# Turning the second 256 tokens of three feature blocks by transposing transfers in place of TensorE transposes

## The chip, the cores and the metric

The kernel runs on one core of a Trainium2 chip. The time is the device time of one execution in microseconds (us), the median of three runs of the kernel before: 1074.78 us (1074.22 to 1075.33).

## The reference

One layer of a residual block for 512 frames of width 1024, all in float32:

```python
for l in range(DEPTH):                                    # DEPTH = 1
    x = x + 0.5 * swiglu(rms_norm(x, ffn1_norm[l]), ffn1_w1[l], ffn1_w3[l], ffn1_w2[l])
    ...                                                   # two token mixers, gates, w_out
    x = x + 0.5 * swiglu(rms_norm(x, ffn2_norm[l]), ffn2_w1[l], ffn2_w3[l], ffn2_w2[l])
return rms_norm(x, final_norm)

def swiglu(h, w1, w3, w2):
    return (jax.nn.silu(h @ w1) * (h @ w3)) @ w2          # 1024 -> 2816 -> 1024
```

The change touches the two SwiGLU stages only: the part that makes `silu(h @ w1) * (h @ w3)`, 2816 features for 512 tokens, and hands it to the product with `w2`.

## The kernel before, in words

**Order of the program.** The first SwiGLU stage fills the first quarter of the execution, the mixers the middle, and the second SwiGLU stage the last quarter. Both stages are one class, `Wide`, so what the change does happens once near 110 to 235 us and once more near 843 to 968 us. Within the stage each engine's instructions run in the order in which the code issues them.

**The wide product.** Of the 2816 features, the first 256 are made apart and the other 2560 in five blocks `b` = 0 to 4 of 512 features. A block is made of seven products `n` = 0 to 6 (a scheme of seven products for a 2 by 2 split of tokens and input rows, with sums of weights taken on the way). A product (b, n) has 24 matrix products of 128 by 512: two halves `h` of the weights, two groups `i` of 128 tokens, two slices `k` of 128 input rows, and three products each, since every float32 operand is split into a rounded part and a rest (`hi` and `lo`). From the third block on the order is (b,0), (b-1,4), (b-1,3), (b,1), (b,2), (b,6), (b,5), and the stage ends with (4,4), (4,3). `m` counts the products in this order.

**Weights.** After half `h` of product `m`, `weight(m + 2, h)` splits the weights of two products later: a cast on ScalarE (ACT) into a ring of four places (`sraw`, `swhi`) and a subtraction on VectorE (DVE) for the rest (`sraw`, `extra`, `swlo`). Then it starts the next transfer into the buffer that was just read: a plain load on SyncE's queue (`cc`, and others), or a load that adds to what is there on GpSimd's queue (POOL).

**Gating and turning.** `finish` combines the products in PSUM into two tiles, `u[0]` for the first 256 tokens and `u[1]` for the second 256, gates them, and leaves 128 tokens on the partitions by 512 features. The product with `w2` (class `Seven`) wants features on the partitions: `hidden(j)`, tiles named `rl` and `rh`. There are two ways to turn:

- *By transfers*: `apart` splits each float32 into its two 16-bit words with two ACT copies (128 by 1024 words) into a scratch tile (`p`, or the silu tile `sa` for the second half), and two transposing DMAs on SyncE's queue write them back, turned, into `u`. `joined` puts the words together with four ACT copies of 128 by 512 words, at the place in the order that `joins` names.
- *By TensorE (PE)*: `turn_half` turns `u[1]` with eight transposes of 128 by 128 into two PSUM banks, and four ACT copies of 128 by 256 take them out.

Before the change the first 256 tokens of blocks 0 to 3 and the second 256 of block 0 go by transfers; the second 256 of blocks 1, 2 and 3 go by `turn_half`, after the first half of (b,2) of the block that follows; block 4 goes by TensorE (`turn`) at the stage's end.

**The stage's end.** During (4,6) and (4,5) ACT and DVE also prepare the first operands of `Seven` from the turned features: `one` casts them, and `second(1)` subtracts `rh` from `rl` for feature tiles 8 to 15, whose second 256 tokens come from blocks 1, 2 and 3. After (4,3), PE turns block 4's `u[0]` and `u[1]` between the first products with `w2`.

In the rows below all of these run through one helper at line 103; tiles tell them apart. In the trace "P" is a PSUM bank.

Of the kernel before, what the change touches and what calls it, by code (L numbers as in the profile page):

```python
# [19 lines left out]
P = 128  # L20
T = 512
# [61 lines left out]
def kernel(  # L83
# [24 lines left out]
    dve, act, pe = [Queued(e, False) for e in (nc.vector, nc.scalar, nc.tensor)]  # L108
# [18 lines left out]
    def tmp(name, shape=(P, T), dt=F32, tag="t", **kw):  # L127
        return tp.tile(list(shape), dt, tag=tag, name=name, **kw)


    ident = cp.tile([P, P], F32, name="ident")
# [42 lines left out]
    def mm3(ps, whi, wlo, xhi, xlo, first, last, onto=False):  # L174
        pe.matmul(ps, whi, xhi, start=first, stop=False, skip_group_check=onto)  # L175
        pe.matmul(ps, whi, xlo, start=False, stop=False, skip_group_check=onto)  # L176
        return pe.matmul(ps, wlo, xhi, start=False, stop=last, skip_group_check=onto)  # L177
# [322 lines left out]
    KH, TH, LO, HI = KF // 2, T // 2, slice(0, D // 2), slice(D // 2, D)  # L500
# [149 lines left out]
    class Wide:  # L650
# [139 lines left out]
                cols = slice(half * TH, (half + 1) * TH)  # L790
                act.copy(s.seven.hidden(2 + 4 * s.end + f)[:, cols], s.turns[f][:, cols])

        def turn_half(s, b):
            for f in range(4):
                for i in range(2):
                    pe.transpose(s.Y[b % 2][f // 2][:, (2 * (f % 2) + i) * P:][:, :P], s.u[1][:, i, f * P:(f + 1) * P], ident[:])
            for f in range(4):
                act.copy(s.seven.hidden(2 + 4 * b + f)[:, TH:T], s.Y[b % 2][f // 2][:, f % 2 * TH:][:, :TH])

        def apart(s, b, half):  # L800
            for i in range(2):
                parts, words = (s.sa if half else s.p[b])[i].bitcast(U16), s.u[half][:, i].bitcast(U16)
                act.copy(parts.rearrange("p (s c) -> p s c", s=2), words.rearrange("p (c s) -> p s c", s=2))
                nc.sync.dma_start(words.rearrange("p (a t) -> p a t", t=P), parts, transpose=True)
# [104 lines left out]
        def blocks(s, pa, pb, more):  # L909
            sv, end, nrm = s.seven, s.end, s.nrm  # L910
            raw = [[t[k][:, 0:TH] for k in range(KD)] for t in (nrm.hi, nrm.lo)]
            soon = {(0, 0): ((s.sums, 1),), (0, 6): ((s.low, 1),), (1, 6): ((s.low, 2),), (0, 1): ((s.low, 4),),
                    (0, 2): ((s.low, 5),), (0, 5): ((s.low, 3),)}
            todo = {(0, 0): ((s.gated, 0),),
                    (1, 0): ((s.cast, 1), (s.sums, 2)),
                    (0, 6): ((s.cast, 2), (s.sums, 4), (s.back, 0)),
                    (1, 6): ((s.cast, 4), (s.sums, 5), (s.hidden, 1, pa[:], pb[:])),
                    (0, 1): ((s.cast, 5), (s.gated, 1)),
                    (0, 2): ((s.cast, 3),),
                    (0, 5): ((s.cast, 0),),  # L920
                    (0, 3): ((s.low, 0), (s.cast, 6)),
                    (1, 2): ((s.low, 6),),
                    (2, 5): ((sv.second, 0),), (3, 2): ((sv.two, 0),),
                    (end, 0): ((sv.operand, 0, 0),), (end, 2): ((sv.operand, 0, 1),), (end, 6): ((sv.one, 0),),
                    (end, 5): ((sv.second, 1), (sv.one, 1)), (end, 4): ((sv.two, 1), *[(s.plain, sv.O[i], s.residual[i]) for i in range(2)])}
            for at, steps in more.items():
                todo[at] = tuple(todo.get(at, ())) + steps
            joins = {}
            for m, (b, n) in enumerate(s.order):
                apart = n == 4 and (b < EARLY or b == end)  # L930
                early = m < 2 * EARLY
                ps = s.X[b % 2] if n in (0, 2, 3, 5) or early else s.X[(b + 1) % 2] if n == 6 or apart else s.Y[b % 2]
                onto = n in (2, 3, 5) or (n == 6 and early) or (n == 4 and not apart)
                last = m + 2 >= len(s.order)
                if last:
                    sv.slots += s.ring[2 * m % 4:2 * m % 4 + 2]
                for h in range(2):
                    wh, wl = s.ring[(2 * m + h) % 4]
                    for i in range(2):
                        for k in range(2):  # L940
                            c = slice(i * P, (i + 1) * P)
                            if early:
                                qh, ql = [t[4 * (n > 0) + 2 * h + k][:, c] for t in raw]
                            else:
                                qh, ql = [t[:, 2 * h + k, c] for t in s.q[n]]
                            mm3(ps[i][:], qh, ql, wh[:, k], wl[:, k], not onto and h + k == 0, h + k == 2, onto)
                    if b > 1 and (n, h) == (2, 0):
                        s.turn_half(b - 1)
                    if h == 1:
                        if m == len(s.order) - 1:  # L950
                            s.turns = dict(zip((0, 2, 1, 3), s.Y[end % 2] + s.X[1 - end % 2]))
                            act.activation(s.sa[0], ps[0][:], AF.Silu)
                            act.activation(s.sa[1], ps[1][:], AF.Silu)
                            s.turn((0, 2), 0)
                            for i in range(2):
                                dve.tensor_tensor(s.u[1][:, i], s.u[1][:, i], s.sa[i], op=ALU.mult)
                            sv.operand(0, 2)
                        else:
                            s.finish(m)
                    if h == 1:  # L960
                        for f, *a in soon.get((b, n), ()):
                            f(*a)
                    if not last:
                        s.weight(m + 2, h)
                    elif len(sv.slots) == 2:
                        sv.weight(0, h)
                    elif h == 0:
                        sv.slots.insert(2, s.last)
                        sv.weight(0, 2)
                        sv.weight(0, 3)  # L970
                    else:
                        sv.weight(0, 4)
                    if (m, h) in joins:
                        s.joined(*joins[m, h])
                if n == 4 and b < end or (b, n) == (0, 3):
                    s.apart(b, int(n == 3))
                    joins[m + 3, 0] = b, int(n == 3)
                s.gate(m)
                for f, *a in todo.get((b, n), ()):
                    f(*a)  # L980
            sv.slots.append(tuple(tmp("g5", (P, 1, T), F32R)[:] for _ in range(2)))
            sv.junk = [tmp(f"osq{i}")[:] for i in range(2)]
            sv.weight(0, 5)
            sv.run()
# [121 lines left out]
    with ExitStack() as mx:  # L1106
# [292 lines left out]
        for t in range(C - 1):  # L1399
            n, m = t + 1, C - 1 - t  # L1400
# [820 lines left out]
```

## Time and profile before

| | before |
|---|---|
| median of three runs | 1074.78 us |
| the profiled execution | 1075.51 us |
| its span, first to last instruction | 1073.8 us |
| PE busy | 1064.3 us (99%) |
| DVE busy | 829.5 us (77%) |
| ACT busy | 706.7 us (66%) |
| POOL busy | 224.5 us (21%) |
| granted TensorE clock | 1.000 |
| DMA traffic | 184.48 MB, mean 172 GB/s |

Stretches of 38 us of the two stages (times from the span's start): from 110 to 148 us PE is busy 38.00 us, DVE 25.75, ACT 24.58, and the DMA engines have a share of 0.93; from 186 to 224 us 38.00, 29.92, 26.04 and 0.84; from 224 to 262 us 37.79, 35.77, 26.34 and 0.97. A share of DMA near or above 1 means that all 16 engines had packets all the time.

How to read the rows: a row of the timeline gives the start, the duration, the engine, the line, the operation, what is written and read, the shape, and in brackets how long the engine stood idle before it and what ended that. SPq is SyncE's queue, and its row is the issue of a transfer. In the view of the DMA engines the window is cut into 40 equal slices, with a digit (tenths busy) and GB/s for each.

### The profile page before, as it was taken

What the parts mean: (1) busy time and instruction counts of PE and PEld (TensorE: products, weight loads), DVE (VectorE), ACT (ScalarE), POOL (GpSimd) and SP (SyncE); (2) the same over time, 40 slices, a digit from 0 to 9 for tenths busy, and PEclk for the clock granted to TensorE, in tenths of its full rate; (3) what the DMA queues carried; (4) which work ended last, traced back from release to release, by engine and by line L of the source; (5) the groups of instructions that cost most, each with busy time, mean ns of one, the idle gap of its engine ahead of it and who ended that gap; (6) DMA issues with size and microseconds to landing.
All of it is one profiled execution on the core that took longest, in us unless ns stands there. A gap on an engine that the chain in (4) does not pass through costs nothing.

```text
span 1073.8 us, 16805 instructions
## 1 busy us (share of the span) xinstructions
PE 1064.3 (99%) x6266; PEld 872.7 (81%) x6266; DVE 829.5 (77%) x1155; ACT 706.7 (66%) x1115; POOL 224.5 (21%) x275
## 2 busy tenths in 40 slices
PE   9999999999999999999999999999999999999997
PEld 7888888888887887888788787888888888888886
DVE  7997676789865698888777777876798766689874
ACT  6768756776555666545888876554578757676654
POOL 1221220134203201412000121135311212114210
PEclk9999999999999999999999999999999999999999
DMA  7989988889945443444312344667979979879972
GB/s 209 264 188 232 226 178 227 196 194 187 233 129 168 116 111 98 129 136 118 89 46 73 100 129 153 188 168 181 290 168 226 196 205 200 201 216 202 233 191 79
DMA packets 171664, 184.48 MB, mean 172 GB/s; under 512 B 41662, under 2 KB 107774, under 8 KB 171582
## 3 DMA queue, kind: packets, MB, share of 16 engines
q1 hardware_dynamic: 137454, 111.82, 35.3%
q0 software_dynamic: 33392, 70.14, 34.1%
q10 hardware_dynamic: 736, 1.45, 0.4%
q8 instruction: 49, 0.80, 0.3%
q14 instruction: 33, 0.27, 0.1%
HBM read 163.51 MB, written 12.52 MB: 164 GB/s over the span
## 4 chain that ended last, share of the span: by engine, by line
PE 78%; issue 12%; DVE 4%; DMA 2%; POOL 2%; ACT 2%; POOLq 0%; DVEq 0%; ACTq 0%; SPq 0%
PE P L103 21%; PE P L175 6%; PE P L176 6%; PE P L177 6%; PE pgt L103 5%; PE l L103 3%; PE spot L103 3%; PE pq L103 3%; PE ppj L103 2%; PE pk L175 2%; PE pk L177 2%; PE pk L176 2%; PE pw L176 1%; PE pw L177 1%; PE pw L175 1%
## 5 line engine op out<-in xcount | busy, mean ns | idle before, releaser
L103 PE MATMUL P<-sraw,q 128*128 128x512 f32 x344 | 91.3, 389 | 0.0
L103 PEld LDWEIGHTS P<-sraw,q 128*128 128x128 f32 x344 | 64.6, 188 | 13.4
L103 PE MATMUL P<-swhi,q 128*128 128x512 f32 x224 | 71.3, 390 | 0.2 <-DVE q L103 0.2
L167 ACT CAST whi<-raw 128x1024 fp32r<-128x1024 f32 (+2 forms) x42 | 40.4, 961 | 43.7 <-issue 14.2
L103 PE MATMUL P<-sraw,wxh 128*128 128x512 f32 x200 | 67.9, 391 | 0.0
L103 PE MATMUL P<-swhi,wxh 128*128 128x512 f32 x144 | 56.8, 394 | 0.0
L103 PE MATMUL P<-swhi,wxl 128*128 128x512 f32 x144 | 56.1, 390 | 0.0
L103 PE MATMUL P<-swlo,wxh 128*128 128x512 f32 x144 | 56.1, 389 | 0.0
L168 DVE TENSOR_TENSOR wlo<-raw,whi 128x1024 fp32r<-128x1024 f32 (+2 forms) x43 | 48.4, 1126 | 9.5 <-ACT whi L167 8.3
L693 POOL DMA_DIRECT2D cb<-in_ffn_w_dram x20 | 24.1, 1207 | 144.8 <-DVE cd L103 77.5
L693 POOL DMA_DIRECT2D cd<-in_ffn_w_dram x24 | 29.3, 1221 | 116.7 <-DVE sraw L103 38.7
L103 PE MATMUL P<-sraw,wxl 128*128 128x512 f32 x136 | 53.0, 389 | 0.0
L103 PEld LDWEIGHTS P<-swhi,q 128*128 128x128 f32 x224 | 41.9, 188 | 9.3 <-DVE q L103 0.6
L103 PEld LDWEIGHTS P<-sraw,wxh 128*128 128x128 f32 x200 | 37.5, 188 | 7.7
L103 PE MATMUL P<-swlo,q 128*128 128x512 f32 x112 | 43.6, 389 | 0.0
L103 ACT COPY RD<-spot 32x128 f32<-32x128 f32 (+2 forms) x128 | 39.8, 311 | 5.3 <-PE spot L103 2.4
L103 DVE TENSOR_TENSOR u<-P,u 128x512 f32<-128x512 f32 x52 | 33.6, 682 | 7.6 <-ACT u L103 7.6
L552 POOL DMA_DIRECT2D ca<-in_ffn_w_dram x16 | 19.3, 1205 | 94.6 <-DVE swlo L103 65.6
L177 PE MATMUL pk<-xh,wlo 128*128 128x512 f32 x96 | 37.5, 392 | 1.0 <-DVE wlo L168 1.0
L175 PE MATMUL pk<-xh,whi 128*128 128x512 f32 x96 | 38.0, 396 | 0.4 <-DVE u L1254 0.4
L176 PE MATMUL pk<-xl,whi 128*128 128x512 f32 x96 | 37.5, 391 | 0.0
L177 PE MATMUL P<-swhi,wxl 128*128 128x512 f32 x96 | 37.3, 389 | 0.0
(630 smaller groups left out, 3432.3 us busy)
## 6 DMA issues: line engine op xcount, KB each, us to landing
raw<-in_w_in_dram SPq DMA_DIRECT2D x40, 512.0 KB
cc<-in_ffn_w_dram SPq DMA_DIRECT2D x36, 512.0 KB
cb<-in_ffn_w_dram POOLq DMA_DIRECT2D x36, 512.0 KB, 6.9
cb<-in_ffn_w_dram SPq DMA_DIRECT2D x32, 512.0 KB
cd<-in_ffn_w_dram POOLq DMA_DIRECT2D x32, 512.0 KB, 7.7
ca<-in_ffn_w_dram POOLq DMA_DIRECT2D x32, 512.0 KB, 8.0
ca<-in_ffn_w_dram SPq DMA_DIRECT2D x20, 512.0 KB
cd<-in_ffn_w_dram SPq DMA_DIRECT2D x18, 512.0 KB
```

Source lines behind the costliest of these rows:

```text
L103: q.last = do(*a, **kw)
L167: (hi_eng or act).copy(hi[:], raw[:])
L168: (eng or dve).tensor_tensor(lo[:], raw[:], hi[:].bitcast(F32), op=ALU.subtract)
L175: pe.matmul(ps, whi, xhi, start=first, stop=False, skip_group_check=onto)
L176: pe.matmul(ps, whi, xlo, start=False, stop=False, skip_group_check=onto)
L177: return pe.matmul(ps, wlo, xhi, start=False, stop=last, skip_group_check=onto)
L552: nc.gpsimd.dma_start(s.sum[g], src, accum_op=ALU.add)
L693: nc.gpsimd.dma_start(to, s.block(b, n, h), accum_op=ALU.add)
```

## The change

`turn_half` and its call go. In its place, for b = 2, 3 and 4, after the first half of (b,1), `apart(b - 1, 1)` issues two ACT copies of `u[1]` into `sa` and two transposing DMAs on SyncE's queue, and `joined(b - 1, 1)` runs three products later, after the first half of (b,5). In each stage this takes 24 transposes off PE and 12 copies of 128 by 256 off ACT, and adds 6 copies of 128 by 1024 words and 12 of 128 by 512 words to ACT and 6 transposing DMAs to SyncE's queue.

```diff
-        def turn_half(s, b):
-            for f in range(4):
-                for i in range(2):
-                    pe.transpose(s.Y[b % 2][f // 2][:, (2 * (f % 2) + i) * P:][:, :P], s.u[1][:, i, f * P:(f + 1) * P], ident[:])
-            for f in range(4):
-                act.copy(s.seven.hidden(2 + 4 * b + f)[:, TH:T], s.Y[b % 2][f // 2][:, f % 2 * TH:][:, :TH])
-
...
-                    if b > 1 and (n, h) == (2, 0):
-                        s.turn_half(b - 1)
...
                     if (m, h) in joins:
                         s.joined(*joins[m, h])
+                    if b > 1 and (n, h) == (1, 0):
+                        s.apart(b - 1, 1)
+                        joins[m + 3, 0] = b - 1, 1
                 if n == 4 and b < end or (b, n) == (0, 3):
                     s.apart(b, int(n == 3))
                     joins[m + 3, 0] = b, int(n == 3)
```

Nothing else moves: on every engine the other instructions keep their order. Three places show what does, all in the last round, b = 4, of the first stage. On ACT, around (4,1) and (4,2), where `swhi<-cc` are the casts of (4,6)'s weights and `sraw<-cb` the cast of (4,5)'s:

```order
 L103 CAST sraw<-cd_380 128x1024
 L103 CAST swhi<-cc_363 128x1024
+L103 COPY sa_455<-u_385 128x1024
+L103 COPY sa_456<-u_385 128x1024
 L103 CAST swhi<-cc_364 128x1024
-L103 COPY rl_372<-P_501 128x256
-L103 COPY rh_375<-P_501 128x256
-L103 COPY rl_373<-P_502 128x256
-L103 COPY rh_376<-P_502 128x256
 L103 CAST sraw<-cb_381 128x1024
```

The four copies out of PSUM are gone, and the two that split words stand one half product earlier, between the two casts. On ACT again, around (4,5), where `wxh<-rl` is an operand for `w2`, `sraw<-cd` the cast of (4,3)'s first half of weights, and `u<-P` takes (4,5) out of PSUM:

```order
 L103 CAST wxh_507<-rl_371 128x1024
 L103 CAST sraw<-cd_379 128x1024
+L103 COPY rl_372<-u_385 128x512
+L103 COPY rh_375<-u_385 128x512
+L103 COPY rl_373<-u_385 128x512
+L103 COPY rh_376<-u_385 128x512
 L103 COPY u_385<-P_495 128x512
 L103 COPY u_385<-P_496 128x512
```

The four copies of `joined` stand ahead of the two that free PSUM after (4,5), and so ahead of all that ACT does up to the stage's end. On SyncE's queue at the same round, the changed kernel's rows (before, the same rows without the two that read `sa`; `u_384<-p` belongs to the first 256 tokens):

```order
L797 DMA_TRANSPOSE u_384<-p_503 128x8x128
L797 DMA_TRANSPOSE u_384<-p_504 128x8x128
L797 DMA_TRANSPOSE u_385<-sa_455 128x8x128
L690 DMA cc_363<-in_ffn_w_dram 128x2x512
L797 DMA_TRANSPOSE u_385<-sa_456 128x8x128
L690 DMA cc_364<-in_ffn_w_dram 128x2x512
L555 DMA cb_381<-in_ffn_w_dram 128x2x512
```

One transposing DMA now stands ahead of each of the two `cc` loads, which bring the weights of (4,4).

## The prediction

> **What bounds the kernel now.** I read the page, then TensorE's waits, then the stretch of the last rounds of blocks, then the rows of ACT, DVE and the DMA engines there. The profiled execution took 1075.51 us, 0.7 us over the median of 1074.78; I sum against its span and put the difference on the median.
>
> ```profile
> span 1073.8 us, 16805 instructions
> PE 1064.3 (99%) x6266; PEld 872.7 (81%) x6266; DVE 829.5 (77%) x1155; ACT 706.7 (66%) x1115; POOL 224.5 (21%) x275
> PE P L103 <- DVE u L103: 0.4, 2, 0.2
> 186.00:224.00 38.00, 38.00 (x174) 31.54 (x173) 29.92 (x32) 26.04 (x36) 4.82 (x4) 1.00 0.84 215
> ```
>
> The rows are from the page, from PE's waits and from the busy times by stretch. PE sets the time: in the last round of the first stage (third number of the window row) it is busy all 38 us. Among its few waits is one by place: twice, once a stage, it waits for DVE's `u`. That is the stage's end, and PE reaches it with nothing to spare. So time taken off PE counts only as far as the stage's end gets earlier too.
>
> **What leaves PE.**
>
> ```profile
> 123.39 1.04 PE L103 MATMUL P<-ident,u 128*128 128x128 f32 x8
> 124.50 0.39 PE L103 MATMUL P<-extra,wxh 128*128 128x512 f32 x1
> 124.73 0.39 PE L103 MATMUL P<-sraw,wxl 128*128 128x512 f32 x1
> L103 PE MATMUL P<-ident,u 128*128 128x128 f32 x40 | 5.8, 274 | 0.2 <-DVE u L103 0.2
> ```
>
> The first three rows are PE's timeline in round b = 2, the last is the group of all transposes of `u` in the first stage. One `turn_half` is eight transposes. From 123.39 to 124.50 lie 1.11 us; one product of the steady pace (124.50 to 124.73, 0.23) is in it, so a call costs 0.88 us. Of the 40 transposes of a stage 24 go: 3 x 0.88 = 2.64 us, in two stages **5.3 us**. That is the gross gain, on the path.
>
> **What ACT loses and gets.**
>
> ```profile
> L103 ACT COPY rh<-P 128x256 f32<-128x256 f32 x10 | 3.7, 386 | 1.2 <-PE P L103 1.2
> L103 ACT COPY sa<-u 128x1024 uint16<-128x1024 uint16 x2 | 2.0, 1055 | 0.0
> L103 ACT COPY rl<-u 128x512 uint16<-128x512 uint16 x10 | 6.9, 692 | 0.0
> 204.14 0.71 ACT L103 COPY rl<-u 128x512 uint16<-128x512 uint16 x1
> 204.71 0.72 ACT L103 COPY rh<-u 128x512 uint16<-128x512 uint16 x1
> ```
>
> These are ACT's groups in the first stage and two rows of its timeline. A round loses four copies of 0.39 us and gets two of about 1.05 and four of 0.69 that follow each other every 0.57 (204.14 to 204.71), so 2.3 us for the four of `joined`. ACT is busy 26 of 38 us, and the weights it casts are for two products later. In the second and third round (b = 2, 3) I cost all of it at nothing: that lead covers it, and if it were gone each round would lose up to the 2.3 us. In the last round there is no such cover.
>
> **The chain at the stage's end.**
>
> ```profile
> 209.48 1.06 ACT L103 CAST swhi<-cc 128x1024 fp32r<-128x1024 f32 x1
> 210.74 1.05 ACT L103 CAST swhi<-cc 128x1024 fp32r<-128x1024 f32 x1 [0.20 <-PE P L103]
> 212.81 1.23 ACT L103 ACTIVATE p<-p 128x512 f32<-128x512 f32 x2 [1.02 <-DVE p L103]
> 214.88 1.05 ACT L103 CAST sraw<-cd 128x1024 fp32r<-128x1024 f32 x1
> 215.83 1.06 ACT L103 COPY u<-P 128x512 f32<-128x512 f32 x2
> 216.78 1.06 ACT L103 CAST sraw<-cd 128x1024 fp32r<-128x1024 f32 x1
> 220.87 1.06 ACT L103 CAST wxh<-rl 128x1024 fp32r<-128x1024 f32 x1 [3.03 <-DVE rl L103]
> 210.96 1.22 DVE L103 TENSOR_TENSOR swlo<-cc,swhi 128x1024 fp32r<-128x1024 f32 x1
> 212.09 1.28 DVE L103 TENSOR_TENSOR p<-P,p 128x512 f32<-128x512 f32 x2
> 218.49 1.21 DVE L103 TENSOR_TENSOR extra<-cd,sraw 128x1024 fp32r<-128x1024 f32 x1
> 219.62 1.22 DVE L103 TENSOR_TENSOR rl<-rl,rh 128x1024 f32<-128x1024 f32 x1
> 221.96 1.23 DVE L103 TENSOR_TENSOR wxl<-rl,wxh 128x1024 fp32r<-128x1024 f32 x1 [1.12 <-ACT wxh L103]
> 231.18 1.28 DVE L103 TENSOR_TENSOR u<-u,sa 128x512 f32<-128x512 f32 x2
> 232.52 0.55 PE L103 MATMUL P<-ident,u 128*128 128x128 f32 x3 [0.21 <-DVE u L103]
> ```
>
> These are the timelines of ACT, DVE and PE in the last round; read them backwards. PE's transposes at 232.52 wait for `u<-u,sa` (231.18 to 232.46). From 221.96 to there DVE has no idle stretch, and at 221.96 it had waited for ACT's `wxh`, which had waited 3.03 us for DVE's `rl<-rl,rh`, ended at 220.84. That follows `extra<-cd`, whose cast ACT makes at 216.78 after the two copies at 215.83. So whatever moves the end of `rl<-rl,rh` moves PE. From the silu at 212.81 to 220.84 it is 8.03 us.
>
> `joined` now stands between 214.88 and 215.83 and moves the cast at 216.78 by 2.3 us. Its end goes from 217.84 to 220.14 on this scale, while DVE was ready for it at 218.49; so 1.65 us are added, and silu to the end of `rl<-rl,rh` becomes 9.7 us.
>
> When can the silu start? By PE's lead and the four PSUM copies that ACT no longer makes (I estimate 0.6 of their 1.5 us), at best 212.81 - 2.64 - 0.6 = 209.5; then `rl<-rl,rh` ends at 219.2, 1.6 us earlier than before, in place of 2.64. ACT keeps its order, however: ahead of the silu stand both casts of `cc`, and these need the loads that now have a transposing DMA in front of each.
>
> **The DMA queue.**
>
> ```profile
> L804 SPq DMA_TRANSPOSE u<-sa x4: 1237/1310/2420, 91.8 to 827.3; - x4
> 198.63 3.09 SPq L690 DMA_DIRECT2D cc<-in_ffn_w_dram  x2
> DMA  0899999999999999999417888679779980006797
> DMA  9999999999999999999989753332122101000009
> DMA  9979997756322312111109198301888998999996
> DMA packets 1676, 0.43 MB, mean 213 GB/s; under 512 B 1673, under 2 KB 1673, under 8 KB 1676
> DMA packets 414, 0.80 MB, mean 398 GB/s; under 512 B 25, under 2 KB 25, under 8 KB 414
> q0 software_dynamic: 544, 1.05, 59.3%
> q1 hardware_dynamic: 2537, 1.36, 52.3%
> q0 software_dynamic: 372, 0.73, 107.5%
> q1 hardware_dynamic: 15, 0.00, 0.6%
> ```
>
> On SyncE's queue a transpose waits for its ACT copy, and the `cc` load, the second transpose, the second `cc` load and then `cb` stand behind it. An issue takes 1.3 us in the median (first row), so `cc` goes out that much later than at 198.63; that is hidden by the time the loads lie in a full queue.
>
> The first DMA row is 190 to 230 us in slices of 1 us: from about 191 to 209 all engines are full. The second (207 to 211, slices of 0.1) thins out from 209.3; I put the end of the second `cc` load at 209.7. The third is the same place of the second stage (942 to 946): thin from 942.8, last packets at 943.9. The `cc` loads are the last of that queue, so what is put ahead of them delays them.
>
> In the last rows q0 is POOL's queue and q1 SyncE's. A transposing DMA moves 128 x 1024 words of 2 bytes, 0.262 MB in 1024 packets of 256 B. The trace has no such transfer at this place, so I bound it. Alone on the engines (155.6 to 157.6 us, the row of 1676 packets) they pass at 213 GB/s: a pair costs 0.524 / 213 GB/s = **2.5 us**. Mixed with adding loads (836 to 848 us; q0 544 packets, q1 2537): the 1.05 MB of q0 take 5.8 us at the pace of 198 to 202 us (372 packets, 0.73 MB in 4 us), the 0.84 MB of q1 that is not turned 2.1 us at the 398 GB/s of plain loads alone (206.9 to 208.9 us), and of 12 us some 4 are left for the pair. From below, at that same 398 GB/s, 1.3 us; nothing at all only if the loads need not wait for it. I take 2.5: the new transposes alternate with plain loads of their own queue, and the adding loads were issued before them.
>
> The Trainium skill (Advanced Engine Details and Errata, X-Bar Transpose) holds that transposing DMAs are as fast as ordinary ones, 350 to 400 GB/s. This trace shows 213. By the page a pair would be an estimated 1.4 us and the sum below -0.5 us.
>
> **The sum.** At (4,1) PE leads by 2 x 0.88 = 1.76, and the queue with it.
>
> First stage: second load at 209.7 - 1.76 + 2.5 = 210.4; its cast of 1.05 ends at 211.5; silu; `rl<-rl,rh` ends 9.7 later at 221.2, against 220.84: **+0.4**.
>
> ```profile
> 943.99 1.05 ACT L103 CAST swhi<-cc 128x1024 fp32r<-128x1024 f32 x1 [0.22 <-PE P L103]
> 952.85 1.22 DVE L103 TENSOR_TENSOR rl<-rl,rh 128x1024 f32<-128x1024 f32 x1
> ```
>
> Second stage: 943.9 - 1.76 + 2.5 = 944.6, the cast ends at 945.7, `rl<-rl,rh` at 955.4, against 954.07: **+1.3**. (Here the load was in time by 0.1 us only.)
>
> So PE gains 2.64 us a stage and waits 3.0 and 3.9 us there: **+1.7 us** in all, 1073.8 to 1075.5 in the span, and **1076.5 us** on the median. With S for the pair's price, the sum is 2S - 3.3 from S of about 1.
>
> **Rivals.**
>
> *The loads are not held up.* If the transposes cost `cc` under 0.6 us, `joined` alone decides: -1.6 in the first stage; in the second 943.9 - 1.76 + 1.05 + 9.7 = 952.9 against 954.07, -1.2. Sum -2.8, **1072.0 us**. For it: with q0 and q1 served in turn, `cc` would pass adding loads. Against it: in the window 198 to 202, with `cc` issued at 198.63, q0 moved 372 packets and q1 nothing but 15 tiny ones. The Trainium skill (DMA: Bandwidth & Descriptors, Queues, rings and completion order) says each engine goes round the queues that have work; by those rows the trace does not show it. Chance 0.22.
>
> *The pair costs what it cost in the mix, 4 us (slower).* Place: (4,1), where two adding loads are in flight when the first transpose is issued, as at 836 us. Then 2 x 4 - 3.3 = +4.7, **1079.5 us**. It is beyond 0.2% from S = 2.7. The Trainium skill (VectorE: DVE Perf Modes, Rules for kernel authors) advises TensorE for turning 128 by 128 where PSUM will do; that rule speaks for this rival, and the priced rows cannot exclude it. Against it: the adding loads are issued first here. Chance 0.26.
>
> *The full gain.* The chain above has slack that I don't see, and all 5.3 us arrive: **1069.5 us**. For it: in every earlier place such transfers were hidden (PE has no gap in the window row above, with such a pair in it). Against it: PE's waits at 232.52 show the chain taut. Chance 0.10.
>
> That PE isn't relieved can be left out: its rows of transposes are gone from the order.
>
> **How the numbers follow.** The forecast, 1076.5 us, has 0.42; its own range is S from 1.3 to 2.9, -0.7 to +2.5, 1074.1 to 1077.3. The range of 8 in 10 runs from 1 us under the first rival, 1071.0, to half a us above the second, 1080.0; left out are the full gain and a price above 4.3 us. A measurement of this kernel tells 0.2%, 2.1 us, from no change. Faster: the full gain 0.10 and two thirds of the first rival, 0.15: 0.25. Slower: the second rival but a little, 0.25, and the top of the forecast's range, 0.05: 0.30. The same: 0.45.
>
> **What would show it.** In the changed profile: PE's steady pace without the eight transposes, and products 0.88, 1.76, 2.64 us earlier after each round; ACT's first cast of `cc` in (4,6) idle before it, waiting for a DMA; `rl<-rl,rh` ending near 221.2 and 955.4; PE's wait for DVE's `u` grown from 0.4 us to some 7 us. If that wait stays under 2 us, the chain or the DMA price is wrong; if PE stalls in (2,4) or (3,4) instead, the cover of the earlier rounds is.

## The result, and the profile after

The changed kernel takes **1085.55 us** (median of 11 runs, 1077.5 to 1089.27); the kernel before, on the same chips, 1074.78 (also of 11). The ratio is 1.0097, with a 95% interval of 1.0077 to 1.0117: slower by some 10.8 us, outside the predicted range of 1071.0 to 1080.0. The runs of the kernel before lie within 1.1 us of each other, those of the changed kernel within 11.8 us. In all that follows, executions more than 1.5% above the fastest of their kernel (two of ten in run 2, two of four in run 5) count as slow: the ratios leave them out, the medians and ranges do not.

The profiled execution of the changed kernel took 1089.27 us, the slowest of the 11, so the trace shows the loss at its largest (3.7 us over the median); the span grew from 1073.8 to 1087.6 us. Its page and its list of PE's waits (us in all, times, longest):

```profile
span 1087.6 us, 16757 instructions
PE 1065.9 (98%) x6218; PEld 871.7 (80%) x6218; DVE 831.6 (76%) x1155; ACT 725.0 (67%) x1127; POOL 224.6 (21%) x275
PE P L103 <- DVE u L103: 6.4, 6, 2.1
PE P L103 <- DVE p L103: 4.1, 1, 4.1
PE pv L176 <- DVE wlo L168: 1.1, 1, 1.1
```

PE executes 48 matrix instructions fewer and is still busy 1.6 us longer. Waits are not the whole story, then: some of PE's work got slower.

Where the time comes in is read from instructions that both kernels have. The next two fences show four of them on PE's timeline, first of the kernel before, then of the changed one: round b = 2 of the first stage, the first product after the first stage, the start of the second stage's rounds, the first product after the second stage.

```profile
98.91 0.39 PE L103 MATMUL P<-sraw,wxh 128*128 128x512 f32 x1
237.48 0.39 PE L103 MATMUL P<-sraw,q 128*128 128x512 f32 x1
821.38 0.39 PE L103 MATMUL P<-sraw,wxh 128*128 128x512 f32 x1
970.71 0.39 PE L103 MATMUL P<-sraw,q 128*128 128x512 f32 x1
```

```profile
98.76 0.39 PE L103 MATMUL P<-sraw,wxh 128*128 128x512 f32 x1
237.60 0.39 PE L103 MATMUL P<-sraw,q 128*128 128x512 f32 x1
823.28 0.39 PE L103 MATMUL P<-sraw,wxh 128*128 128x512 f32 x1
984.24 0.39 PE L103 MATMUL P<-sraw,q 128*128 128x512 f32 x1
```

Between the first two the changed kernel loses 138.84 - 138.57 = 0.3 us, between the second and third (the middle of the program, which the change does not touch) 1.8 us, and between the last two, the second stage, **11.6 us**. The same three differences are taken of every run below.

**The second stage.** The waits of over 1 us on PE's timeline there, and the granted clock behind them (stretch, its length, PE's busy time and instructions, granted clock, share of the DMA engines, GB/s):

```profile
918.07 0.50 PE L103 MATMUL P<-swhi,q 128*128 128x512 f32 x1 [2.14 <-DVE u L103]
956.71 0.77 PE L103 MATMUL P<-swhi,q 128*128 128x512 f32 x1 [4.09 <-DVE p L103]
972.09 0.33 PE L103 MATMUL P<-ident,u 128*128 128x128 f32 x1 [1.36 <-DVE u L103]
918.00:920.00 2.00, 1.93 (x5) 0.62 1.08 265
920.00:922.00 2.00, 2.00 (x6) 0.52 1.08 313
922.00:924.00 2.00, 2.00 (x10) 1.00 1.05 404
956.00:958.00 2.00, 1.29 (x3) 0.51 1.07 395
958.00:960.00 2.00, 2.00 (x6) 0.50 0.95 285
960.00:962.00 2.00, 2.00 (x7) 0.50 0.91 350
962.00:964.00 2.00, 2.00 (x9) 0.78 1.02 411
972.00:974.00 2.00, 1.63 (x7) 0.78 0.80 92
974.00:976.00 2.00, 2.00 (x7) 0.50 0.99 176
976.00:978.00 2.00, 2.00 (x11) 0.87 0.92 136
```

The waits are 2.14 + 4.09 + 1.36 = 7.6 us. Behind each, PE's clock is at half: 6 or 7 instructions in 2 us in place of 10 or 11. PE's busy time in these stretches times the missing share of the clock is 0.73 + 0.96 + 0.63 + 1.00 + 1.00 + 0.44 + 0.36 + 1.00 + 0.26 = 6.4 us. With the 2.6 us that PE saves, 7.6 + 6.4 - 2.6 = 11.4 of the 11.6 us.

What the two longer waits hang on is seen on ACT and DVE (timelines, stage 2), and on the queues of POOL and SyncE at the last round of both stages (issues: start, time on the queue):

```profile
914.26 0.68 ACT L103 COPY rl<-u 128x512 uint16<-128x512 uint16 x1 [2.78 <-DMA u<-sa]
953.66 1.04 ACT L103 CAST swhi<-cc 128x1024 fp32r<-128x1024 f32 x1 [8.23 <-DMA cc<-in_ffn_w_dram]
956.02 1.05 ACT L103 CAST swhi<-cc 128x1024 fp32r<-128x1024 f32 x1 [1.32 <-DVE swlo L103]
954.74 1.23 DVE L103 TENSOR_TENSOR swlo<-cc,swhi 128x1024 fp32r<-128x1024 f32 x1 [7.86 <-ACT swhi L103]
955.88 1.28 DVE L103 TENSOR_TENSOR p<-P,p 128x512 f32<-128x512 f32 x2
965.55 1.22 DVE L103 TENSOR_TENSOR rl<-rl,rh 128x1024 f32<-128x1024 f32 x1
```

```profile
196.38 2.19 SPq L797 DMA_TRANSPOSE u<-sa  x1
199.48 5.86 SPq L797 DMA_TRANSPOSE u<-sa  x1
935.58 1.20 POOL L693 DMA_DIRECT2D cd<-in_ffn_w_dram  x1 [1.13 <-DVE extra L103]
935.68 2.71 SPq L797 DMA_TRANSPOSE u<-sa  x1
938.49 2.37 SPq L690 DMA_DIRECT2D cc<-in_ffn_w_dram  x1
940.91 8.73 SPq L797 DMA_TRANSPOSE u<-sa  x1
949.74 0.56 SPq L690 DMA_DIRECT2D cc<-in_ffn_w_dram  x1
```

In the second stage ACT's first cast of `cc` in (4,6) waits 8.23 us for its load; DVE's `swlo<-cc` waits for that cast, `p<-P,p` stands behind it, and PE's 4.09 us end with the first `p`. A round earlier `joined` waits 2.78 us for its transposed words, and the copies out of PSUM stand behind it: that is the wait of 2.14 us. The first `cc` load was issued at 938.49, behind the first transpose, and landed 15.1 us later, 2.1 us after that transpose. On SyncE's queue the second transpose takes 8.73 us to issue, and the second `cc` load goes out only behind it, at 949.74: 11.3 us after the first. It landed at 955.92, and until 955.97 DVE was at work for the first load's weights, so the late landing of the first load by itself explains PE's 4.09 us. In the first stage the second transpose takes 5.86 us to issue. How fast the DMA engines moved at these two places (windows of the changed kernel; granted clock, share of the DMA engines, GB/s):

```profile
200.00:202.00 2.00, 1.00 1.12 203
204.00:206.00 2.00, 1.00 1.20 174
942.00:944.00 2.00, 1.00 1.37 89
944.00:946.00 2.00, 1.00 1.44 93
946.00:948.00 2.00, 1.00 1.47 77
948.00:950.00 2.00, 1.00 0.89 79
```

The engines are busy nearly all the time at both places (a share of 0.89 or more). In the first stage they move some 170 to 200 GB/s, in the second 77 to 93 for 8 us. In these 8 us, called the collapse below, a transposing transfer and an adding load of POOL are in flight together: the adding load that was issued at 935.58 landed 16.9 us later, the transpose of 935.68 after 15.8 us.

### The profile page after: what moved, and what is told of

Read it like the earlier page. It is cut to its first block, busy times and chain, and to the rows that moved or that the text cites. A ratio compares the mean times of both kernels' runs of the same rounds, so it can differ in the third digit from the quotient of the medians.

```text
span 1087.6 us, 16757 instructions
## 1 busy us (share of the span) xinstructions
PE 1065.9 (98%) x6218; PEld 871.7 (80%) x6218; DVE 831.6 (76%) x1155; ACT 725.0 (67%) x1127; POOL 224.6 (21%) x275
## 4 chain that ended last, share of the span: by engine, by line
PE 83%; DMA 5%; DVE 5%; ACT 4%; issue 2%; SPq 0%; POOL 0%; DVEq 0%; ACTq 0%; POOLq 0%
PE P L103 30%; PE P L176 5%; PE P L177 5%; PE P L175 5%; PE pgt L103 5%; PE l L103 3%; PE spot L103 3%; PE pq L103 3%; DMA cc<-in_ffn_w_dram 2%; PE ppj L103 2%; PE pk L175 2%; PE pk L177 2%; DMA u<-sa 2%; PE pk L176 2%; PE pw L176 1%
## 5 line engine op out<-in xcount | busy, mean ns | idle before, releaser
L103 PE MATMUL P<-swhi,q 128*128 128x512 f32 x224 | 74.8, 406 | 6.5 <-DVE p L103 4.1
L103 PEld LDWEIGHTS P<-swhi,q 128*128 128x128 f32 x224 | 44.2, 198 | 17.2 <-issue 4.5
L103 PE MATMUL P<-swhi,wxl 128*128 128x512 f32 x144 | 56.5, 393 | 0.0
L103 DVE TENSOR_TENSOR swlo<-cc,swhi 128x1024 fp32r<-128x1024 f32 x20 | 24.5, 1224 | 21.3 <-ACT swhi L103 20.8
```

The source lines that it names most:

```text
L103: q.last = do(*a, **kw)
```

## Experiments

Two theories stood against each other. A: the new transfers hold up the loads that stand behind them, and PE waits for these. B: ACT's new copies come between its casts and set the end. The differences in the table are those of the four rows above, each run's against the kernel before's, in its profiled execution; medians are of 4 to 11 runs.

| kernel | median, us (range) | ratio (95%) | stage 1 | middle | stage 2 |
|---|---|---|---|---|---|
| changed | 1085.55 (1077.5-1089.3) | 1.0097 (1.0077-1.0117) | +0.3 | +1.8 | +11.6 |
| 1 without the new transfers | 1073.7 (1072.4-1075.5) | 0.9988 (0.9978-0.9998) | -1.7 | +1.8 | -1.5 |
| 2 blocks 1, 2 by transfers, 3 on PE | 1073.18 (1071.0-1091.9) | 0.9985 (0.9973-0.9997) | -1.7 | +1.6 | -0.1 |
| 3 block 3 alone by transfers | 1082.11 (1081.4-1082.5) | 1.0067 (1.0052-1.0082) | +2.7 | +2.1 | +2.7 |
| 4 a product later | 1078.05 (1077.9-1079.8) | 1.0033 (1.0020-1.0046) | +0.3 | +1.5 | +1.2 |
| 5 in effect the change again | 1100.0 (1083.3-1110.9) | none | +1.8 | +3.3 | +12.6 |
| 6 in effect 2 again | 1073.32 (1072.2-1076.9) | 0.9993 (0.9983-1.0003) | -1.8 | +1.6 | -1.8 |
| 7 kernel before with a wait | 1086.37 (1085.2-1087.7) | 1.0109 (1.0094-1.0124) | +5.8 | +0.1 | +5.3 |
| 8 as 2, PE padded | 1074.32 (1073.9-1075.7) | 0.9999 (0.9990-1.0009) | -0.2 | 0.0 | -0.2 |
| 9 behind the loads | 1074.08 (1073.2-1077.0) | 0.9995 (0.9986-1.0004) | -1.4 | +2.0 | -1.5 |
| 10 as 9, block 3 on PE | 1072.06 (1071.0-1073.2) | 0.9975 (0.9965-0.9985) | -1.8 | +0.6 | -1.8 |
| 11 as 10, PE padded | 1073.2 (1072.4-1074.0) | 0.9985 (0.9976-0.9994) | -0.8 | +0.1 | -0.8 |
| 12 transposes later by a copy | 1080.46 (1079.6-1081.7) | 1.0054 (1.0037-1.0070) | +0.5 | +1.3 | +2.5 |

**1: without the new transfers.**

```diff
-                nc.sync.dma_start(words.rearrange("p (a t) -> p a t", t=P), parts, transpose=True)
+                if move:
+                    nc.sync.dma_start(words.rearrange("p (a t) -> p a t", t=P), parts, transpose=True)
...
-                        s.apart(b - 1, 1)
+                        s.apart(b - 1, 1, False)
```

> The changed kernel without its new transposing transfers: both ACT copies of `apart` and the four of `joined` stay, `joined` reads u[1] as it stands (so the second half of three blocks is not turned, and its values are wrong). Theory A (the new transfers hold up the loads that stand behind them, and PE waits for these): 1070 to 1073 us, near the 1072.0 of the rival 'the loads are not held up', and no PE wait over 2 us. Theory B (ACT's new copies come between the casts and set the end): the time stays near that of the change, 1080 us or more. If PE's relief were worth nothing: 1075.

1073.7 us: theory A. ACT's six copies per round are there, and still the two stages come out 1.7 and 1.5 us shorter. So the transfers cost the 11.9 us between this run and the change, and ACT's copies don't. It is a little over the range expected, 1070 to 1073, for the middle takes 1.8 us back (below).

**2 and 3: which rounds.** In the one, round b = 4 keeps `turn_half`; in the other, rounds 2 and 3 do.

```diff
+                    if b > 1 and not (b < end) and (n, h) == (2, 0):
+                        s.turn_half(b - 1)
...
-                    if b > 1 and (n, h) == (1, 0):
+                    if b > 1 and (b < end) and (n, h) == (1, 0):
```

> Blocks 1 and 2 (rounds b = 2, 3) turned by transfers as in the change, block 3 (round b = 4) on PE as before. If only the last round is without cover, as the prediction had it: 2 x 0.88 us a stage stay, 1071.3 us. If round b = 3 is hit too, as the changed kernel's trace shows with PE's wait of 2.14 us before 918.07: 1074 to 1080 us, with more spread from run to run than the kernel before.

> Only block 3 (round b = 4) by transfers, blocks 1 and 2 on PE as before. If the last round alone makes the loss: 1080 us or more, nearly all that the change loses. If the loss is shared over the rounds: 1076 to 1080.

1073.18 and 1082.11 us. The last round alone loses 7.3 us (2.7 in each stage and 2.1 in the middle), two thirds of the change's loss, steadily; rounds 2 and 3 gain on balance (eight of the ten executions from 1071.0 to 1077.2). In the profile of run 3 the transposes go out 0.66 us behind the adding load in both stages, and the engines do not fall below 100 GB/s: the first ones land in 9.9 and 10.1 us. What it loses is the stage's end, twice, with the half clock behind waits of 1.91 and 2.19 us.

**4: a product later.** `apart` after (b,2) h = 0, both `cc` loads ahead of the transposes.

```diff
-                    if b > 1 and (n, h) == (1, 0):
+                    if b > 1 and (n, h) == (2, 0):
                         s.apart(b - 1, 1)
-                        joins[m + 3, 0] = b - 1, 1
+                        joins[m + 2, 0] = b - 1, 1
```

> `apart` one product later, after (b,2) h = 0, so that on SyncE's queue both `cc` loads go out ahead of the transposes and POOL's adding loads are nearly done when these are moved; `joined` stays where it is. Theory A: the loads go out as before, 1071 to 1074 us, PE's waits at the stage's end under 2 us. Theory B (ACT's copies, which stay the same): 1080 us or more. If the transposes are too late for `joined`: ACT waits for DMA u<-sa before (b,5) and the time is over 1076.

1078.05 us: neither theory's number. The third case, transposes too late for `joined`, is not it either: ACT nowhere waits for them. The executions lie within 1.9 us, but PE waits 2.14 and 2.12 us at the stages' ends. `apart`'s two ACT copies now stand at 202.56, ahead of the copies out of PSUM and of the `cc` casts, and the silu starts at 210.63 (209.30 in run 1). Place of the transfers and place of the copies had to be told apart.

**5 and 6: an attempt that changed nothing.** The copies were to stay where the change has them, and the transfers to be issued after (b,2) h = 0.

```diff
+                    if b > 1 and (n, h) == (1, 0):
+                        s.apart(b - 1, 1, send=False)
+                    if b > 1 and (n, h) == (2, 0):
+                        s.apart(b - 1, 1, copy=False)
+                        joins[m + 2, 0] = b - 1, 1
```

> As the run with the transfers behind the loads, but only the transfers come one product later (after (b,2) h = 0, behind both `cc` loads); `apart`'s two ACT copies stay after (b,1) h = 0. There these copies stood between the casts and put the silu 1.3 us later in each stage. If that was what the later place lost: 1073 to 1075.5 us, the silu in the first stage near 209.3 (as in the run without transfers) and PE's waits at the stage's end under 1.5 us. If the transfers delay the end from any place: 1077 us or more.

> Blocks 1 and 2 by transfers behind the loads (copies after (b,1) h = 0, transfers after (b,2) h = 0), block 3 on PE. If the spread of the kernel with blocks 1 and 2 by transfers ahead of the loads (1071.0 to 1091.9) came from transposes that share the DMA engines with adding loads: 1071 to 1073 us with all runs within 3 us. If the spread stays, its cause is another.

1100.0 us (1083.3 to 1110.9) and 1073.32 (1072.2 to 1076.9). Neither tests its theory. Nothing in the code ties these transfers to the loads, and in the built program they stand where they stood; SyncE's queue in run 5:

```profile
195.79 1.96 SPq L799 DMA_TRANSPOSE u<-sa  x1
197.85 0.92 SPq L690 DMA_DIRECT2D cc<-in_ffn_w_dram  x1
```

So run 5 repeats the change and run 6 repeats run 2, in the same order of every engine. What they show is the spread of one and the same order: the change and run 5 together from 1077.5 to 1092.8 us, runs 2 and 6 from 1071.0 to 1077.2, without the four executions that the ratios leave out.

**7: a wait without a transfer.** The kernel before, with eight ACT copies ahead of the silu in (4,6):

```diff
                 for t in s.p[b]:
+                    for _ in range(4 if b == s.end else 0):
+                        act.copy(t, t)
+                for t in s.p[b]:
                     act.activation(t, t, AF.Silu)
```

> The kernel before, with eight copies of p onto itself (128x512, about 0.57 us each) put ahead of the silu in (4,6) of each stage: 4.6 us of ACT on the chain of the stage's end, and nothing on the DMA side; the result stays the same. If a wait costs its length alone: two PE waits of about 4.5 us, 1083.8 us, granted clock 1.00 throughout. If PE's clock falls to half after a wait of over 2 us, as the changed kernel's trace shows from 956.04: 1.7 to 3.4 us more in each stage, 1087 to 1091 us.

The wait came out shorter than meant. PE's timeline and a window behind it:

```profile
229.61 0.33 PE L103 MATMUL P<-ident,u 128*128 128x128 f32 x1 [3.19 <-DVE u L103]
232.00:234.00 2.00, 2.00 (x9) 0.50 0.75 133
```

Two waits of 3.19 us should make about 1081 us; it took 1086.37, and the clock is at half for 3.41 us after each. The stages lost 5.8 and 5.3 us, so a wait at this place costs its length and 2.1 to 2.6 us more, with no transfer involved.

**8: as many PE instructions as before.** As run 6 (in effect run 2), with eight dummy transposes in each of the two rounds:

```diff
                         s.apart(b - 1, 1, copy=False)
+                        for f in range(8):
+                            pe.transpose(s.Y[(b - 1) % 2][f // 4][:, 8 * (f % 4):][:, :8], ident[0:8, :], ident[0:8, 0:8])
```

> As the run with blocks 1 and 2 by transfers behind the loads and block 3 on PE, but PE does eight dummy transposes of 128x8 in the two rounds, so that it executes as many instructions as the kernel before. If the wait of 1.0 to 1.4 us at pv<-wlo (465 us), which all changed kernels have and the kernel before has not, comes from where the fetch of PE's instructions (16 KB, one packet) falls beside the load raw<-in_w_in: that wait is gone, the load lands 3.9 us after its issue and not 5.4, and the time is at or under that of the kernel without the dummies although these cost PE up to 0.5 us each round. If the wait stays, it has another cause.

The wait at `pv<-wlo` is gone and the middle's difference is 0.0. The dummies cost all that PE had saved (stage 1 -0.2 in place of -1.8), so the time is 1.0 us over that of run 6, not at or under it as expected. In the load `raw<-in_w_in` before that wait, 15 of its 16 shares land within 4.0 us of the issue in both kernels; the last took 5.34 us in the changed one and 3.95 in this one (3.88 in the kernel before).

**9: behind the loads, copies early.** The transfers are tied to the last load:

```diff
+                if send:
+                    with ExitStack() if copy else tc.issue_after(loads[-1].ins):
+                        sent = nc.sync.dma_start(words.rearrange("p (a t) -> p a t", t=P), parts, transpose=True)
+                    if not copy:
+                        loads.append(sent)
...
+                    if b > 1 and (n, h) == (1, 0):
+                        s.apart(b - 1, 1, send=False)
+                    if b > 1 and (n, h) == (1, 1):
+                        s.apart(b - 1, 1, copy=False)
+                        joins[m + 3, 0] = b - 1, 1
```

> All three blocks by transfers; `apart`'s ACT copies after (b,1) h = 0 as in the change, its two transfers tied behind both `cc` loads (after (b,1) h = 1), so that on SyncE's queue the order is cc, cc, transpose, transpose, cb, cb. The silu of the first stage comes near 209.3 as in the run without transfers, and PE's waits at the stage's end fall under 1.5 us each: 1073 to 1075.5 us with runs within 3 us of each other, if the change's loss is that the transposes meet the adding loads and hold up `cc`. If the transfers delay the end from any place: 1077 us or more, or a spread as wide as the change's.

1074.08 us: **11.5 us come from where two DMA issues of a round stand**. SyncE's queue in the last round of the second stage, two DMA windows there, ACT's silu of the first stage and PE's waits for `u`:

```profile
930.41 3.21 SPq L690 DMA_DIRECT2D cc<-in_ffn_w_dram  x2
933.67 7.08 SPq L800 DMA_TRANSPOSE u<-sa  x2
936.00:938.00 2.00, 1.00 1.08 269
940.00:942.00 2.00, 1.00 1.60 107
209.31 1.23 ACT L103 ACTIVATE p<-p 128x512 f32<-128x512 f32 x2 [0.39 <-DVE p L103]
PE P L103 <- DVE u L103: 1.8, 6, 0.4
```

Both `cc` loads go out in 3.2 us, the silu starts at 209.31 (the prediction had 209.5 as the best), and PE's longest wait for `u` is 0.4 us. The transposes still take 7.1 us to issue, but only `cb` is behind them. The engines slow down here too, to 107 GB/s at 940 to 942, but for 2 us, and when the second `cc` load lands at 940.97. The transposes now go out 3.9 to 4.3 us behind the last adding load, so this run changes that distance along with the order on the queue. Both stages gain 1.4 to 1.5 us; the middle takes 2.0 back.

**10 and 11: the best of both.** As run 9, with block 3 on PE as before; and the same with four dummy fp32 matmuls of 1x1 in each of the two rounds.

```diff
+                    if b > 1 and b < end and (n, h) == (2, 0):
+                        for f in range(4):
+                            pe.matmul(s.Y[(b - 1) % 2][f // 2][0:1, f:f + 1], ident[:, 0:1], ident[:, 0:1], start=True, stop=True)
```

> Blocks 1 and 2 by transfers tied behind both `cc` loads, block 3 on PE. PE gains 4 x 0.88 = 3.5 us, of which 1.0 to 1.4 go to the wait at pv<-wlo: 1072.3 to 1073 us, all runs within 3 us. If the spread of the kernel with blocks 1 and 2 by transfers ahead of the loads (up to 1091.9) stays, it does not come from transposes and adding loads side by side.

> As the run before this, with four dummy fp32 matmuls of 1x1 in each of the two rounds, so that PE executes as many instructions as in the kernel before, at some 0.2 us a round. If the wait at pv<-wlo comes with the place of the instruction fetch: that wait is gone and the time is 1071 to 1072 us, 0.5 to 1 us under the run before this. If the fetch is not its cause: 1073 to 1074 us with the wait in place.

Run 10 takes 1072.06 us, 0.25% under the kernel before (interval 0.15 to 0.35%): it beats both kernels. Both stages gain the full 2 x 0.88 = 1.76 us that PE no longer spends. The padded run is slower, 1073.2, against expectation: its middle is as before (+0.1), but the dummies cost about 1.0 us a stage, and in the profile of run 10 the middle lost only 0.6, with no wait at `pv<-wlo`.

**12: later by a copy.** The first transposes went out 0.1 to 0.7 us behind the second adding load in the changed kernel; one more ACT copy moves them further behind.

```diff
                     if b > 1 and (n, h) == (1, 0):
+                        act.copy(s.u[1][:, 0], s.u[1][:, 0])
                         s.apart(b - 1, 1)
```

> The changed kernel with one more ACT copy (u[1], 128x512 onto itself, about 0.57 us) ahead of `apart`'s copies in rounds b = 2, 3, 4, so that each first transpose goes out some 0.6 us later; the order on SyncE's queue stays transpose, cc, transpose, cc. In the profiles so far a first transpose that is issued 0.66 to 0.70 us after the second adding load lands 9.7 to 11.2 us later, one at 0.36 us or less up to 15.8 us later, and the adding load itself takes up to 16.9 us in place of some 9 to 12. If that distance decides the collapse: first transposes land in 9 to 12 us everywhere, no 2 us under 100 GB/s, 1078 to 1081 us with runs within 4 us of each other (what stays is the hold-up of `cc`, the wait at the stage's end and the half clock behind it). If the collapse has another cause: 1083 to 1090 us and a spread as wide as the change's.

1080.46 us with four runs within 2.1 us, the time expected if that distance decides: 5.1 us less than the change for one copy **more** on ACT. The order on SyncE's queue is the change's in rounds 3 and 4; in round 2 one `cc` load now goes out ahead of both transposes. The transposes go out 1.0 to 1.35 us after the adding load; the first ones land in 8.7 to 12.5 us (9 to 12 expected), the adding loads take 9.2 to 11.7. SyncE's queue in the last round of the second stage:

```profile
932.17 2.45 SPq L797 DMA_TRANSPOSE u<-sa  x1
934.72 1.63 SPq L690 DMA_DIRECT2D cc<-in_ffn_w_dram  x1
936.40 3.71 SPq L797 DMA_TRANSPOSE u<-sa  x1
```

The second transpose holds the queue for 3.71 us (8.73 in the change). Two windows of 2 us are still under 100 GB/s (95 at 942 to 944, 54 at 864 to 866); it was expected that none would.

Does the distance decide? Over all runs with transposes beside the adding loads (the change, 2, 3, 5, 6, 8 and 12), 17 first transposes were issued within 0.4 us of an adding load: five took 13.7 to 15.8 us, the adding load 16.0 to 16.9, all in rounds 3 and 4 of the second stage; twelve took 9.8 to 13.0. The 15 that were issued 0.66 to 1.35 us behind took 8.7 to 12.5. So all that took over 13 us were issued close to an adding load, but most of the close ones did not take that long: a small distance goes with the collapse and does not suffice for it, and what else is needed stays open.

## Why the prediction was wrong

**PE's saving** was right. Runs 10 and 6 show it undisturbed: -1.8 us a stage with two blocks turned by transfers (2 x 0.88 = 1.76).

**The chain at the stage's end** was right, and the first stage came out as worked out. The timelines of ACT and DVE in the changed kernel:

```profile
211.13 1.15 ACT L103 ACTIVATE p<-p 128x512 f32<-128x512 f32 x2
219.72 1.22 DVE L103 TENSOR_TENSOR rl<-rl,rh 128x1024 f32<-128x1024 f32 x1
```

From the silu to the end of `rl<-rl,rh` it is 9.8 us (9.7 forecast); that end is 220.94 (221.2 forecast), and the first stage's loss 0.3 us (+0.4 forecast). PE's wait is 2.06 us, at 226.26: it comes at the first of the stage's last transposes, not at the one of 232.52. Run 1, without the transfers, gives the rival "the loads are not held up" stage by stage: -1.7 and -1.5 us against -1.6 and -1.2.

**The step that failed is the price of the pair of transposes** (S = 2.5 us, bounds 1.3 to 4), as one number for both stages. In the first stage the second `cc` load landed at 210.08; from 209.67 in the kernel before, less the 1.76 us of lead and 0.15 of an earlier start, that is S = 2.3. In the second it landed at 955.92; from 943.89 less 1.76 and plus the 1.9 us by which the stage began later, S = 11.9, three times the upper bound. The chain behind the load held here too: 955.92 + 1.05 + 9.7 = 966.7, and `rl<-rl,rh` ended at 966.77 (forecast 955.4). The upper bound came from the one place where transposes and adding loads were seen together (836 to 848 us). The reason given against a higher price, "the adding loads are issued first here", was no protection: in that round the first transpose went out 0.1 us behind an adding load and took 15.8 us, the adding load 16.9, and the engines fell to 77 to 93 GB/s. In the last rounds of run 12, 1.3 us behind, the same reckoning gives S = 2.6 and 2.8, within the bounds. That the transfers ahead of the loads make the loss is shown by runs 1 and 9; that a small distance goes with the highest price, by the runs together; it does not suffice, and what passes inside the DMA engines is not shown.

**The queue** was half right. An issue was costed at 1.3 us, "hidden by the time the loads lie in a full queue". The second transpose held SyncE's queue for 5.3 to 9.1 us in rounds 2 to 4, and the second `cc` load behind it was not in the queue at all. In the second stage the first load, which was in the queue, was late enough by itself. Run 9 shows what transposes ahead of the loads cost in all, 11.5 us; run 12, with that order kept in rounds 3 and 4 and no first transpose over 12.5 us, takes 6.4 us longer than run 9, with one ACT copy more a round.

**Rounds b = 2, 3 at nothing** held in the first stage and failed in the second: PE waited 2.14 us at 918.07. What gave way was not the cover of ACT's 2.3 us, but that `joined` waited 2.78 us for transposes that landed 16.7 us after their issue, with the PSUM copies of the next product behind it.

**A cost that was not in the sum: PE's clock.** The forecast let PE wait 7 us and counted 7 us. The half clock behind the waits added 6.4 us in the second stage of the changed kernel; run 7 shows it without any transfer. It is the larger part of the miss: the stage lost 11.6 us in place of 1.3, and of these 10.3 us the longer waits (7.6 in place of 3.9) are 3.7 and the clock is 6.4. With the 1.8 us of the middle that is nearly all of the 12.1 us by which the profiled span, 1087.6, is over the forecast's 1075.5. Run 12 shows it from the other side: with its S the sum 2S - 3.3 gives 2.1 us, some 1077 us, and it took 1080.46; the half clock behind one wait (3.41 us, so 1.7 lost) and the middle (1.3) are most of the difference. The Trainium skill (TensorE: Matmul & The Clock Gate, HAM oscillation) warns of PE idle gaps over about 3.4 us, after which the array runs at half its clock. The trace agrees on the half, which lasts 3.41 or 6.83 us here. It differs on the gap: 1.36, 1.91, 2.12 and 2.14 us were enough, while waits of 2.06 us (changed kernel, 226.26) and of 2.14 and 2.31 us (runs 4 and 12, first stage) were not followed by it.

**The middle**, 1.8 us, was in no term either. Such a loss (0.6 to 3.3 us) appears in every kernel whose PE executes fewer instructions than before, with or without new transfers, and is 0.1 or less in the three that execute as many up to there (7, 8, 11). In the changed kernel a packet of 16 KB of the queue that fetches instructions starts 1.2 us after the issue of the load `raw<-in_w_in` at 451.09, takes 1.44 us, and one of that load's 16 shares lands 1.4 us after the others; in the kernel before that packet starts 0.4 us ahead of the issue, and all shares land together. That the count of PE's instructions decides is shown by run 8 (and 11); that the late share is one that met the fetch is inferred from the times. In those three and the kernel before, the packet starts 0.29 to 0.43 us ahead of the issue and no share is late; in the other ten it starts between 0.21 us ahead and 3.4 us behind, and the last share is 0.6 to 1.8 us late.

Of the rivals, "the pair costs what it cost in the mix" had the sign and the mechanism (transposes and adding loads side by side at (4,1)) but 4 us where the second stage showed 11.9.

## What to carry to other kernels

A transfer that nothing waits for soon is still not free: on a queue it stands ahead of loads that something does wait for, so put it behind the last load that is due first and tie it there, since code order alone did not. Price a new transfer for the moment at which it is issued, and look at what else the DMA engines do in that microsecond; one price from a quiet place does not carry over. A new wait of 2 us on PE can cost nearly 4, though some here cost only their length, and a gain of 2 us in a program of this length can be eaten by something as far away as where the instruction fetches fall.

## What was not expected of the hardware

- Transposing transfers beside adding loads of POOL took the 16 DMA engines, busy nearly all the time, from some 170 to 200 GB/s to 77 to 93 GB/s for 8 us, and an adding load from 9.7 us at the first of these places to 16.9. Every transposing transfer that took over 13 us was issued within 0.4 us of an adding load, but most that were issued so close took less. The Trainium skill (Advanced Engine Details and Errata, X-Bar Transpose) gives 350 to 400 GB/s for such transfers; no run here shows that.
- The issue of a second transposing transfer held its queue until the first was nearly through: 8.73 us where the first transfer took 15.8, 3.71 where it took 8.7. In all these rounds the issue ended 0.5 to 2.8 us before the first transfer had landed.
- PE's clock falls to half after waits of 1.4 to 2.2 us in some places and not in others, for 3.41 us or twice that (behind the wait of 4.09 us).
- The queue that the page calls instruction moves 49 packets of 16 KB in the changed kernel, and between two of them PE starts some 255 instructions. They go through the engines that carry the loads; 16 instructions fewer in a stage (run 3: 8 transposes with their weight loads) came with 2.1 us lost between the stages, where nothing had been changed.
